# Whole-head probability-value products, PSUM tiles read when complete, and a new planned order in a two-layer attention and mLSTM trunk

## The chip, the cores and the metric

The kernel runs on one core of one Trainium2 chip. The metric is device time in microseconds (us), the median of three runs. The profile is of one execution; its span runs from the first to the last instruction on the core.

The engines are named as the profile names them: PE (TensorE, matmuls), PEld (its weight loads), DVE (VectorE), ACT (ScalarE), POOL (GpSimd) and SP (SyncE, which issues most of the transfers).

## What is computed

Two layers over 512 positions of width 1024. Each layer normalises its input, makes one combined projection and runs two branches from it; the output projection and the residual follow. Cut to what matters here:

```python
q = rope(rmsnorm(two_map_heads(aq), q_norm_g), cos, sin)      # 8 heads, two maps each, 64 wide
k = rope(rmsnorm(two_map_heads(ak), k_norm_g), cos, sin)
...
sc = jnp.einsum('bhqrd,bhkrd->bhrqk', qb, k) * scale           # per block of 128 queries
p = jax.nn.softmax(jnp.where(causal, sc, -jnp.inf), axis=-1)
a = p[:, :, 0] - lam * p[:, :, 1]
oa = jnp.einsum('bhqk,bhkd->bhqd', a, v)                       # v is 128 wide per head
oa = rmsnorm(oa, attn_norm_g) * (1.0 - lam_init) * jax.nn.silu(az)
ya = oa @ w_out_a
...                                                            # mLSTM branch: hb, yb
u = jax.nn.sigmoid(ga) * ya + jax.nn.sigmoid(gb) * yb
return x + u @ w_o
```

## The kernel before

**Number format.** A float32 operand is split into a high part and a remainder (ACT copies the high part, DVE subtracts it: `split`). A product of two such operands is three matmuls: high times high, high times remainder, remainder times high.

**Pieces and chains.** The weight products run as a list of pieces (`TUNE["order"]`): `qk` (queries and keys, four pairs of heads `c`), `av` (values), `az`, `ga`, `bo` and so on, mostly 512 columns wide. Around them stand chains of small steps: for each attention head `attn_head`, for each mLSTM head `ml_head`. Tiles of the profile carry these names: `qkt` are the transposed queries and keys of one pair and one block of 128 positions (four transposes into one PSUM tile, `qk_back`), `sc` the scores, `p` the probabilities, `ut` the transposed probabilities, `uh` and `ul` their high part and remainder, `msp` the sum of squares.

**A head's value products.** In the kernel before, `attn_head` makes them in two halves. `av(0)` covers query blocks 0 and 1 and `av(1)` blocks 2 and 3. Each product is 256 columns wide, and on the diagonal 128. The mLSTM products `num` are already made over the whole head, 512, 384, 256 and 128 columns wide for the four key blocks.

**Who sets the order.** The code does not issue its instructions in the order in which it is written. `Recorder.add` records each instruction with the earlier ones that it must follow. `Recorder.schedule` then plays a list scheduler over all engines, with a table of costs and a key for each instruction, and emits them in the planned order. Each engine runs its own instructions strictly in that order. The waits are then put in by the tile framework for the order that it was given. What the recorder does not know as a dependence, the scheduler may place in any order.

PSUM tiles come from small pools: one tile each for `tr` (all transposes, and the sums `msp`, `den`), `sc` (one of two banks) and `av`, four for the products of the pieces. A sum of squares or a denominator is added over the partitions with a matmul of ones: over two parts (high, remainder), or, for heads in `foldA`, `foldM` or `foldD`, over one part after the upper 64 partitions have been added onto the lower by DVE.

Of the kernel before, what the change touches and what calls it, by code (L numbers as in the profile page):

```python
# [18 lines left out]
P = 128  # L19
# [35 lines left out]
    "slack": 4130.0,
    "margin": 60.0,
    "pemargin": 48.4,
    "wait": 333.1,
    "swpen": 99746.2,
    "smargin": 0.2,  # L60
    "pwait": 2.0,
    "wdiff": 5762.0,
# [9 lines left out]
    "acl": 14,  # L72
    "gateA": 7,
    "gateM": 4,
    "actp": (0, 1, 2, 3),
    "m0": 217,
    "mp": 15,
    "m4": 17,
    "slots": 20,
    "bias": {'av': 11500.0, 'msp_a': -4400.0, 'wl': 2550.0, 'wo': -3700.0, 'mk': 6300.0, 'woh': -4650.0, 'wob': -850.0, 'bv': 2450.0, 'ht': 4400.0, 'woa': -1700.0, 'taz': -5550.0, 'sbo': -8700.0, 'wh': 7950.0, 'ga': -3100.0, 'ulZ': 7100.0, 'gt': -2650.0, 'qs': -5450.0, 'rq': -4050.0, 'p': -850.0, 'uz': -2750.0, 'x': -1750.0, 'ua': 5400.0, 'sdh': -3800.0, 'fo_b': -3100.0, 'lneps': 3350.0, 'wo1_P': 14300.0, 'qkt': -450.0, 'ml': 1700.0, 'den': -1900.0, 'sq': 3050.0, 'ulA': 10450.0, 'uhY': 1850.0, 'wo0_P': -850.0, 'cv': -2300.0, 'ulB': 8050.0, 'ob': 1850.0, 'gw': -150.0, 'out_0_dram': -3650.0, 'qss': 3500.0, 'gb': 100.0, 'xr': 1400.0, 'x1d': 5100.0, 'sinv': 5300.0, 'msl_a': 2200.0, 'p5_wo': -4150.0, 'saz': 3700.0, 's1_wo': 550.0, 'hh': -2400.0, 'mql': 1750.0, 'ulY': 9700.0, 'msp_b': 1200.0, 'em': -6750.0, 'sbz': -4900.0, 'wr': -2400.0, 'xn': 3500.0, 'posi': -500.0, 'ms': 12650.0, 'rot': 1400.0, 'sums': -1100.0, 'wt0_wo': 2350.0, 'mq': 650.0, 'uy': 100.0, 'qt': 5650.0, 'msh_d': 1700.0, 'gf': 1850.0, 'warm': -1450.0, 'ctab': 4550.0, 'gct': -4200.0, 'hl': 150.0, 'fo_a': 350.0, 'ones': 2100.0, 'fb_a': -700.0, 'ut': 450.0, 'ld': 5350.0, 'ang': -1900.0, 'mx': 5650.0, 'dq': 2300.0, 'uh': -500.0, 'gm': -550.0, 'fb_d': 1400.0, 'zeroc': 6400.0, 'gft': -100.0, 'bqk': 2050.0, 'gcol': -1000.0, 'oa': 500.0, 'sdl': 4250.0, 'uhB': 5750.0, 'tbz': 1150.0, 'cosv': 500.0, 'sc': 150.0, 'gi': 6100.0, 'msh_a': 400.0, 'uhA': 250.0, 'ss': 400.0, 'bo': 2500.0, 'posf': 2100.0, 'eps': -6650.0, 'fo_d': -2950.0, 'ws0_wo': -200.0, 'msh_b': -350.0, 'qk0_2x': 150.0, 'msl_d': -3500.0, 'junk': -900.0, 'epsc': 3000.0, 'fb_b': -100.0, 'kl': 1100.0, 'ks': -1450.0, 'msl_b': 200.0, 'ng': 550.0, 'rows': 150.0, 'gc': -150.0, 'qk1_0x': -500.0, 'qk1_2x': 100.0, 'stab': 650.0},  # L80
    "drain": 689.4,
    "risk": 335.5,
    "late": 278.0,
# [19 lines left out]
class Recorder:  # L103
# [61 lines left out]
    def add(self, eng, e, fn, a, k):  # L165
# [6 lines left out]
        for kind, aps in (("r", ins), ("w", outs)):  # L172
            for ap in aps:
                name, quad, mask = self.region(ap)
                ws, rs = self.acc.setdefault(name, ([], []))
                if kind == "r" and ap.space == PSUM:

                    for j, q, m in rs:
                        if self.ops[j]["eng"] != eng:
                            preds.setdefault(j, 0)  # L180
                if kind == "w":
                    for j, q, m in rs:
                        if q & quad and m & mask and j != i:
                            preds.setdefault(j, 0)
                    rs[:] = [x for x in rs if x[0] != i and (x[1] & ~quad or x[2] & ~mask)]
                for j, q, m in ws:
                    if q & quad and m & mask and j != i:
                        preds[j] = 1
                if kind == "w":
                    ws[:] = [x for x in ws if x[0] != i and (x[1] & ~quad or x[2] & ~mask)]  # L190
                    ws.append((i, quad, mask))
                else:
                    rs.append((i, quad, mask))
                t = self.tiles.get(name)
                if t is not None and (not t["ops"] or t["ops"][-1] != i):
                    t["ops"].append(i)
# [246 lines left out]
def kernel(ctx, tc, x, pos, wp, wg, cst, par, pb, ngb, out):  # L443
# [180 lines left out]
    def layer_events(l):  # L624
# [200 lines left out]
        def qk_done(c, tt, acc):  # L825
            if tt == 0:
                names = ("qs0", "qs1", "ks0", "ks1")
                if c % 2 == 0:
                    until(lambda: c == 0 or st.get(("A", 1), 0) > 6)
# [93 lines left out]
        def az_done(m, acc):  # L923
            if m > 1:
                until(lambda: st.get(("A", m - 2), 0) > 10)
            g = gp.tile([P, S], F32, tag="gate", name=f"saz{l}_{m}")
            silu2(g, acc, f"taz{l}_{m}")
            st[("az", m)] = g

        def bo_done(m, acc):  # L930
            until(lambda: st.get(("A", 6 + m), 0) > 10 if m < 2 else st.get(("M", m - 2), 0) > 5)
# [11 lines left out]
        def ga_done(m, acc):  # L943
            if "ua" not in st:
                until(lambda: st.get(("A", 5), 0) > 6)
                st["ua"] = big.tile([P, 8, S], F32, tag="big", name=f"ua{l}")
# [208 lines left out]

        def attn_head(h, t0):
# [33 lines left out]
            def tr(j):  # L1190
                pp, jj, n = j // 2, j % 2, P * (j + 1)
                if jj == 0:
                    loc["uh", pp] = t5([P, 4, 256], f"uh{l}_{h}_{pp}", F32R)
                    loc["ul", pp] = t5([P, 4, 256], f"ul{l}_{h}_{pp}", F32R)
# [3 lines left out]
                cs = slice(jj * P, (jj + 1) * P)  # L1198
                split(loc["uh", pp][:, : j + 1, cs], loc["ul", pp][:, : j + 1, cs], pst[:, : j + 1, :])

            def av(pp):
                if pp == 0:
                    loc["av"] = ps_av.tile([P, S], F32, tag="av", name=f"av{l}_{h}")
                o = loc["av"]
                uh, ul = loc["uh", pp], loc["ul", pp]
                kd = 2 * pp + 1
                c0 = 256 * pp

                def vv(k):
                    v = st[("av", g, k)]  # L1210
                    cs = slice((h % 4) * P, (h % 4) * P + P)
                    return v[:, 0, cs], v[:, 1, cs]

                full = list(range(kd))
                seq = []
                for k in full:
                    vh, vl = vv(k)
                    seq += [(vh, uh[:, k, :], 0), (vh, ul[:, k, :], 0), (vl, uh[:, k, :], 0)]
                vh, vl = vv(kd)
                dgn = [(vh, uh[:, kd, P:256], P), (vh, ul[:, kd, P:256], P), (vl, uh[:, kd, P:256], P)]  # L1220
                seq = seq[:1] + dgn + seq[1:]
                for i, (a, b, off) in enumerate(seq):
                    T.matmul(o[:, c0 + off : c0 + 256], a, b, start=i == 0, stop=i == len(seq) - 1, skip_group_check=True)
                if pp == 1 and h % 4 == 3:
# [12 lines left out]
            def msq():  # L1237
# [3 lines left out]
            fns = [lambda: qk(0), lambda: qk(1), lambda: tr(0), lambda: qk(2), lambda: tr(1), lambda: av(0), lambda: qk(3), lambda: tr(2),  # L1241
                   lambda: tr(3), lambda: (av(1), msq()), fin]

            def need(i):
                if i in (0, 1, 3, 6) and st.get(("qkn", c), 0) < (1, 2, 0, 3, 0, 0, 4)[i]:
                    return False
                if i == 5 and (("av", g, 3) not in st or st.get(("A", h - 1), 11) < 11):
                    return False
                return not (i == 10 and (("az", h) not in st or not room(1)))
# [47 lines left out]
        OFF = (0, 512, 1024, 896)  # L1297

        def ml_head(h, t0):
# [95 lines left out]
            def need(i):  # L1395
# [4 lines left out]
                if i == 4 and (("bv", grp, 3) not in st or st.get(("M", h - 1), 6) < 6 or st[("A", 7)] < 11):  # L1400
# [244 lines left out]
```

## Time and profile before

| | |
|---|---|
| median of 3 runs | 1344.62 us (1344.2 to 1345.06) |
| the profiled execution | 1344.67 us, of which the span is 1342.9 us |
| PE busy | 1331.3 us (99%), 6300 matmuls |
| DVE busy | 1012.6 us (75%) |
| ACT busy | 904.7 us (67%) |
| chain that ended last | PE 98%, ACT 1% |
| granted TensorE clock | 0.999 of full speed over the span |

A matmul's recorded duration overlaps with its neighbour's, so a product's cost is read from the distance between two starts. A row of the timeline gives the start, the duration, what ran, how many, and in brackets the idle time before it with what ended that.

### The profile page before, as it was taken

How to read it: one execution, taken by the hardware profiler on the slowest of the kernel's cores; microseconds unless marked ns; L12 is line 12 of the kernel's file. 1: busy time of each engine (PE TensorE's matmuls, PEld its weight loads, DVE VectorE, ACT ScalarE, POOL GpSimd, SP SyncE). 2: the span in 40 equal slices, each digit the busy share in tenths (PEclk: the TensorE clock that was granted, in tenths of full speed). 3: DMA queues.
4: the chain of work that ended last, by engine and by line, in shares of the span. 5: the costliest groups of instructions: out<-in, count | busy, mean ns of one | idle time of the engine just before them, and what ended most of it. 6: DMA issues, size and time to landing. Idle time of an engine off the chain costs nothing.

```text
span 1342.9 us, 17724 instructions
## 1 busy us (share of the span) xinstructions
PE 1331.3 (99%) x6300; PEld 1100.0 (82%) x6300; DVE 1012.6 (75%) x1806; ACT 904.7 (67%) x1828; POOL 36.9 (3%) x44
## 2 busy tenths in 40 slices
PE   8999999999999999999999999999999999999998
PEld 7787878888888888888888888788888888888887
DVE  7888988786549958755888888887754698587386
ACT  5787888885438858733668787888743488586243
POOL 1000000000000000000200000000000000000010
PEclk9999999999999999999999999999999999999999
DMA  5222222323244433455933122222322434434366
GB/s 186 87 79 64 79 78 64 94 77 101 91 119 112 132 108 114 137 136 146 265 104 97 53 95 63 79 63 94 99 82 91 120 107 135 128 109 140 121 190 172
DMA packets 51274, 148.17 MB, mean 110 GB/s; under 512 B 6096, under 2 KB 12880, under 8 KB 51184
## 3 DMA queue, kind: packets, MB, share of 16 engines
q1 hardware_dynamic: 48880, 138.63, 33.7%
q0 software_dynamic: 2304, 8.39, 3.5%
q8 instruction: 50, 0.82, 0.3%
q14 instruction: 40, 0.33, 0.1%
HBM read 142.74 MB, written 4.26 MB: 109 GB/s over the span
## 4 chain that ended last, share of the span: by engine, by line
PE 98%; ACT 1%; DMA 0%; DVE 0%; issue 0%; SPq 0%; DVEq 0%
PE qk L439 13%; PE av L439 9%; PE az L439 7%; PE ga L439 7%; PE bv L439 7%; PE bo L439 7%; PE bz L439 7%; PE woa L439 7%; PE gb L439 7%; PE bqk L439 7%; PE wob L439 6%; PE wo_P L439 6%; PE sc L439 3%; PE num L439 2%; PE ms L439 1%; PE ut L439 1%
## 5 line engine op out<-in xcount | busy, mean ns | idle before, releaser
L439 ACT CAST wh<-wr 128x1024 fp32r<-128x1024 f32 (+1 forms) x206 | 214.9, 1045 | 195.8 <-PE woa L439 37.7
L439 DVE TENSOR_TENSOR wl<-wr,wh 128x1024 fp32r<-128x1024 f32 x204 | 249.0, 1221 | 108.5 <-ACT wh L439 105.7
L439 PE MATMUL qk<-wl,hh 128*128 128x512 f32 x256 | 94.1, 398 | 0.7 <-DVE wl L439 0.7
L439 PE MATMUL qk<-wh,hl 128*128 128x512 f32 x256 | 93.8, 400 | 0.1
L439 PE MATMUL qk<-wh,hh 128*128 128x512 f32 x256 | 93.3, 399 | 0.6 <-ACT hh L439 0.6
L439 PE MATMUL woa<-oa,wh 128*128 128x512 f32 x256 | 88.5, 391 | 0.0
L439 PE MATMUL wob<-ob,wh 128*128 128x512 f32 x256 | 83.4, 389 | 0.0
L439 ACT ACTIVATE p<-sc,mx,rq 128x128 f32<-128x128 f32 (+3 forms) x128 | 78.9, 618 | 6.5 <-DVE mx L439 6.0
L438 ACT ACT_TABLE_LOAD x61 | 78.3, 1283 | 1.1
L439 PEld LDWEIGHTS qk<-wl,hh 128*128 128x128 f32 x256 | 47.9, 188 | 10.6 <-DVE wl L439 1.2
L439 PEld LDWEIGHTS wob<-ob,wh 128*128 128x128 f32 x256 | 48.1, 188 | 10.0
L439 PEld LDWEIGHTS qk<-wh,hl 128*128 128x128 f32 x256 | 48.0, 188 | 9.7 <-DVE hl L439 0.4
L439 PEld LDWEIGHTS woa<-oa,wh 128*128 128x128 f32 x256 | 47.8, 188 | 9.7
L439 PEld LDWEIGHTS qk<-wh,hh 128*128 128x128 f32 x256 | 47.7, 188 | 9.5 <-ACT hh L439 0.9
L439 DVE TENSOR_REDUCE mx<-sc 128x2 f32<-128x256 f32 (+1 forms) x64 | 52.5, 821 | 0.9
L439 PE MATMUL az<-hh,wl 128*128 128x512 f32 x128 | 51.3, 401 | 0.0
L439 PE MATMUL az<-hl,wh 128*128 128x512 f32 x128 | 50.9, 398 | 0.0
L439 PE MATMUL ga<-hh,wl 128*128 128x512 f32 x128 | 50.6, 398 | 0.0
L439 PE MATMUL ga<-hh,wh 128*128 128x512 f32 x128 | 50.5, 395 | 0.0
L439 PE MATMUL az<-hh,wh 128*128 128x512 f32 x128 | 50.5, 397 | 0.0
L439 PE MATMUL ga<-hl,wh 128*128 128x512 f32 x128 | 50.4, 394 | 0.0
L439 PE MATMUL woa<-oa,wl 128*128 128x512 f32 x128 | 50.0, 391 | 0.0
(314 smaller groups left out, 3737.7 us busy)
## 6 DMA issues: line engine op xcount, KB each, us to landing
wr<-in_wp_dram SPq DMA_DIRECT2D x204, 512.0 KB, 3.6
ws_wo<-in_wp_dram POOLq DMA_DIRECT2D x12, 512.0 KB, 6.6
dd<-rows SPq DMA_DIRECT2D x16, 256.0 KB, 4.9
em<-rows SPq DMA_DIRECT2D x16, 256.0 KB, 3.9
dd<-rows SPq DMA_DIRECT2D x16, 192.0 KB, 5.4
x<-in_x_dram SPq DMA_DIRECT2D x4, 512.0 KB, 8.5
dd<-rows SPq DMA_DIRECT2D x16, 128.0 KB, 6.2
ws_wo<-in_wp_dram SPq DMA_DIRECT2D x4, 512.0 KB
```

Source lines behind the costliest of these rows:

```text
L438: self.tc.keep_in_program_order(self.nc.scalar.preload_act_table_set(self.SET_NAME[o["load"]]))
L439: self.tc.keep_in_program_order(getattr(o["e"], o["fn"])(*o["a"], **o["k"]))
```

## The change

Four things change.

1. In `Recorder.add`, an instruction that reads a PSUM tile now follows every product or transpose recorded so far for that bank of the tile, whatever part of it is read.
2. `attn_head` makes a head's value products once for the whole head, as `num` does: four key blocks of 512, 384, 256 and 128 columns, three matmuls each. `uh` and `ul` are one tile per head. The last block's transposes are copied out in two pieces.
3. Sets in `TUNE`: head 6 leaves `foldA`, all heads are in `foldD`, the scaling of `p` for query block 1 moves from ACT to DVE (`actp`), and the first four pieces split their remainder in two halves (`wsp`).
4. Nearly every number of `TUNE` that feeds the scheduler changes, among them the list of pieces, and so does the order on all engines.

```diff
-    "attn": (1, 5, 5, 8, 9, 10, 12, 16, 16, 19, 24),
+    "attn": (1, 5, 5, 8, 9, 13, 15, 16, 19, 24),
...
-    "pemargin": 48.4,
+    "pemargin": 171.8,
...
-    "wsp": 0,
+    "wsp": 4,
...
-    "foldA": (2, 3, 5, 6),
+    "foldA": (2, 3, 5),
     "foldM": (0, 1, 2, 3, 4, 7),
-    "foldD": (0, 1, 3, 5, 6),
+    "foldD": (0, 1, 2, 3, 4, 5, 6, 7),
...
-    "actp": (0, 1, 2, 3),
+    "actp": (0, 2, 3),
...
                 for j, q, m in ws:
-                    if q & quad and m & mask and j != i:
+
+                    whole = kind == "r" and ap.space == PSUM and any((m >> b) & 0xFFFF and (mask >> b) & 0xFFFF for b in (0, 16))
+                    if (whole or q & quad and m & mask) and j != i:
                         preds[j] = 1
...
             def tr(j):
...
+                uh, ul = (loc[n].rearrange("p (b c) -> p b c", c=P) for n in ("uh", "ul"))
+                bs = slice(j, j + 3 * min(j, 2) + 1, 3)
+                split(uh[:, bs, :], ul[:, bs, :], pst[:, : min(j, 2) + 1, :])
+                if j == 3:
+                    split(uh[:, 7, :], ul[:, 7, :], pst[:, 3, :])
+
+            def av():
+                loc["av"] = o = ps_av.tile([P, S], F32, tag="av", name=f"av{l}_{h}")
+                seq = []
+                for k in range(NT):
                     v = st[("av", g, k)]
                     cs = slice((h % 4) * P, (h % 4) * P + P)
+                    us = slice(OFF[k], OFF[k] + S - P * k)
+                    vh, vl, uh, ul = v[:, 0, cs], v[:, 1, cs], loc["uh"][:, us], loc["ul"][:, us]
+                    seq += [(k, vh, uh), (k, vh, ul), (k, vl, uh)]
+                seq = seq[:1] + seq[2:] + seq[1:2]
+                for q, (k, a, b) in enumerate(seq):
+                    T.matmul(o[:, P * k :], a, b, start=q == 0, stop=q == len(seq) - 1, skip_group_check=True)
+                if h % 4 == 3:
                     give(4)
```

The first place is on PE in layer 0: the four transposes of `qkt0_1_1` (layer 0, pair 1, block 1). Before:

```order
L439 MATMUL av0_1_272<-ul0_1_1_308,av0_0_3_209 128x128
L439 MATMUL av0_1_272<-uh0_1_1_307,av0_0_3_209 128x128
L439 MATMUL qkt0_1_1_312<-ct_94,rot0_1_1_287 128x128 [waits DVE_49,PE_49]
L439 MATMUL qkt0_1_1_312<-ct_94,rot0_1_1_287 128x128 x2
L439 MATMUL qkt0_1_1_312<-ct_94,rot0_1_1_287 128x128 [waits Activation_49]
L439 MATMUL sc0_2_0_322<-kl10_1_281,qs10_1_277 128x128 [waits Pool_49]
```

And now:

```order
L441 MATMUL av0_1_314<-uh0_1_257,av0_0_2_208 128x256
L441 MATMUL av0_1_314<-ul0_1_258,av0_0_2_208 128x256
L441 MATMUL qkt0_1_1_307<-ct_94,rot0_1_1_286 128x128 [waits DVE_49,PE_49]
L441 MATMUL qkt0_1_1_307<-ct_94,rot0_1_1_286 128x128 x3
L441 MATMUL sc0_2_0_318<-kl10_1_280,qs10_1_276 128x128 [waits Pool_49]
```

The fourth transpose no longer waits for ACT: all four stand together behind one wait.

The second place is on PE in layer 0, the value products of head 5 (`av0_5`; behind the arrow stand the probabilities and the values of one key block). Before, the second half of the head:

```order
L439 MATMUL av0_5_551<-uh0_5_1_577,av0_1_0_371 128x256 [waits Activation_49]
L439 MATMUL av0_5_551<-uh0_5_1_577,av0_1_3_381 128x128
L439 MATMUL ga0_4_595<-hl0_115,wh36_574 128x512
L439 MATMUL ga0_4_595<-hh0_114,wl36_575 128x512
L439 MATMUL av0_5_551<-ul0_5_1_578,av0_1_3_381 128x128 [waits DVE_49]
L439 MATMUL av0_5_551<-uh0_5_1_577,av0_1_3_381 128x128
L439 MATMUL av0_5_551<-ul0_5_1_578,av0_1_0_371 128x256
L439 MATMUL av0_5_551<-uh0_5_1_577,av0_1_0_371 128x256
L439 MATMUL av0_5_551<-uh0_5_1_577,av0_1_1_372 128x256
L439 MATMUL av0_5_551<-ul0_5_1_578,av0_1_1_372 128x256
L439 MATMUL av0_5_551<-uh0_5_1_577,av0_1_1_372 128x256
L439 MATMUL av0_5_551<-uh0_5_1_577,av0_1_2_373 128x256
```

And now, the whole head but its first product:

```order
L441 MATMUL av0_5_568<-uh0_5_531,av0_1_0_364 128x512
L441 MATMUL av0_5_568<-uh0_5_531,av0_1_1_365 128x384
L441 MATMUL az0_7_590<-hl0_115,wh36_564 128x512
L441 MATMUL av0_5_568<-ul0_5_532,av0_1_1_365 128x384 [waits DVE_49]
L441 MATMUL av0_5_568<-uh0_5_531,av0_1_1_365 128x384
L441 MATMUL av0_5_568<-uh0_5_531,av0_1_2_366 128x256
L441 MATMUL av0_5_568<-ul0_5_532,av0_1_2_366 128x256
L441 MATMUL av0_5_568<-uh0_5_531,av0_1_2_366 128x256
L441 MATMUL av0_5_568<-uh0_5_531,av0_1_3_375 128x128 [waits Activation_49]
L441 MATMUL av0_5_568<-ul0_5_532,av0_1_3_375 128x128 [waits DVE_49]
L441 MATMUL av0_5_568<-uh0_5_531,av0_1_3_375 128x128
L441 MATMUL av0_5_568<-ul0_5_532,av0_1_0_364 128x512
```

Eighteen products in two groups have become twelve in one, with waits for ACT and DVE at the start of the group and again at its last key block.

## Rows read from the trace of the kernel before

**Rows 1.** The page: the span, the busy time of three engines (share, instructions) and the chain that ended last, by engine.

```profile
span 1342.9 us, 17724 instructions
...
PE 1331.3 (99%) x6300; PEld 1100.0 (82%) x6300; DVE 1012.6 (75%) x1806; ACT 904.7 (67%) x1828; POOL 36.9 (3%) x44
...
PE 98%; ACT 1%; DMA 0%; DVE 0%; issue 0%; SPq 0%; DVEq 0%
```

**Rows 2.** The waits of PE: for whom, us in total, times, the longest.

```profile
PE qkt L439 <- ACT qk_2x L439: 1.8, 4, 0.5
PE qkt L439 <- ACT qs L439: 1.8, 4, 0.5
...
PE qkt L439 <- ACT qk_0x L439: 0.5, 1, 0.5
```

**Rows 3.** The timeline of PE and ACT around one such wait (`qkt` of layer 0, pair 2, block 1).

```profile
181.00 0.49 PE L439 MATMUL qkt<-ct,rot 128*128 128x128 f32 x3
181.53 0.36 ACT L439 CAST qk_2x<-qkt 64x256 fp32r<-64x256 f32 x1 [0.93 <-PE qkt L439]
...
181.94 0.33 PE L439 MATMUL qkt<-ct,rot 128*128 128x128 f32 x1 [0.45 <-ACT qk_2x L439]
```

**Rows 4.** The timeline of PE at two groups of `qkt` with other products between their transposes (pair 1, block 0; pair 3, block 0): the third and the fourth transpose of each. Two 512-column products stand between the two rows of either pair.

```profile
107.81 0.27 PE L439 MATMUL qkt<-ct,rot 128*128 128x128 f32 x1
...
108.68 0.30 PE L439 MATMUL qkt<-ct,rot 128*128 128x128 f32 x1
...
220.33 0.27 PE L439 MATMUL qkt<-ct,rot 128*128 128x128 f32 x1
...
221.06 0.33 PE L439 MATMUL qkt<-ct,rot 128*128 128x128 f32 x1
```

**Rows 5.** The timeline of PE at value products of head 7, layer 0, in two stretches with nothing else between them: six products (three of 256 columns, three of 128), then ten (two of 128 columns, eight of 256). Shown are the first and the last row of each and what follows.

```profile
296.93 0.34 PE L439 MATMUL av<-uh,av 128*128 128x256 f32 x2
...
297.50 0.28 PE L439 MATMUL av<-uh,av 128*128 128x256 f32 x1
297.62 0.39 PE L439 MATMUL bv<-wl,hh 128*128 128x512 f32 x1
...
307.58 0.22 PE L439 MATMUL av<-ul,av 128*128 128x128 f32 x1
...
308.63 0.28 PE L439 MATMUL av<-uh,av 128*128 128x256 f32 x1
308.75 0.40 PE L439 MATMUL woa<-oa,wh 128*128 128x512 f32 x1
```

**Rows 6.** The same view of the mLSTM products `num` of head 7, layer 0: twelve in one stretch, three each of 512, 384, 256 and 128 columns. The first and the last row, and what follows.

```profile
560.16 0.80 PE L439 MATMUL num<-sdh,bv 128*128 128x512 f32 x3
...
561.78 0.45 PE L439 MATMUL num<-sdl,bv 128*128 128x512 f32 x1
562.07 0.62 PE L439 MATMUL wob<-ob,wh 128*128 128x512 f32 x2
```

**Rows 7.** The chain that ended last, in order of time: an undisturbed stretch of 512-column products (start, us, what).

```profile
998.17 8.61 PE bqk L439 x38
```

**Rows 8.** Timeline of PE, ACT and DVE: the shortest reuse of the PSUM tile `tr`, from a transpose through its two copies to the next transpose.

```profile
727.45 0.30 PE L439 MATMUL ut<-ct,p 128*128 128x128 f32 x1
...
727.78 0.27 ACT L439 CAST uh<-ut 128x128 fp32r<-128x128 f32 x1 [1.06 <-PE ut L439]
...
728.13 0.28 DVE L439 TENSOR_TENSOR ul<-ut,uh 128x128 fp32r<-128x128 f32 x1
...
728.61 0.38 PE L439 MATMUL ut<-ct,p 128*128 128x128 f32 x2
```

**Rows 9.** Groups of instructions by line, engine and operation: count, busy us and mean ns, then the idle time before them.

```profile
L439 ACT CAST wh<-wr 128x1024 fp32r<-128x1024 f32 (+1 forms) x206 | 214.9, 1045 | 195.8 <-PE woa L439 37.7
L439 DVE TENSOR_TENSOR wl<-wr,wh 128x1024 fp32r<-128x1024 f32 x204 | 249.0, 1221 | 108.5 <-ACT wh L439 105.7
...
L438 ACT ACT_TABLE_LOAD x61 | 78.3, 1283 | 1.1
...
L439 ACT ACTIVATE p<-p,sums 128x256 f32<-128x256 f32 x16 | 8.2, 512 | 2.3 <-DVE sums L439 2.3
...
L439 ACT CAST uh<-ut 128x384 fp32r<-128x384 f32 x16 | 7.6, 475 | 2.0 <-PE ut L439 2.0
...
L439 ACT COPY fb_d<-dd 64x512 f32<-64x512 f32 x10 | 6.2, 620 | 6.1 <-DVE dd L439 5.9
...
L439 DVE TENSOR_TENSOR dd<-dd,fb_d 64x512 f32<-64x512 f32 x10 | 6.8, 681 | 0.0
...
L439 DVE TENSOR_TENSOR rot<-rot,rq 128x256 f32<-128x256 f32 x16 | 6.7, 420 | 0.3
...
L439 DVE TENSOR_TENSOR ul<-ut,uh 128x128 fp32r<-128x128 f32 x16 | 4.6, 287 | 2.5 <-ACT uh L439 2.5
```

**Rows 10.** Busy time of each engine in the attention stretch of layer 0 (from and to in us, its length, then PE, PEld, DVE, ACT, POOL, the granted clock, the DMA share and GB/s).

```profile
45.00:180.00 135.00, 133.95 (x675) 110.00 (x674) 118.86 (x265) 108.11 (x291) 2.85 (x3) 1.00 0.23 72
```

**Rows 11.** The timeline of PE at the start of the program: the first products that wait for a remainder, and a transpose that waits for the normalised input.

```profile
10.67 0.50 PE L439 MATMUL qk<-wl,hh 128*128 128x512 f32 x1 [0.27 <-DVE wl L439]
...
12.87 0.63 PE L439 MATMUL ht<-ct,junk 128*128 128x128 f32 x4 [0.40 <-DVE junk L439]
...
14.58 0.50 PE L439 MATMUL qk<-wl,hh 128*128 128x512 f32 x1 [0.41 <-DVE wl L439]
```

More of the change, by code (lines that the diff above doesn't have):

```diff
@@ L71 @@
     "prods": 'P1 P5 P3 P6 P2 P7 P4',
[L72 to L76 removed]
+    "acl": 12,
+    "gateA": 9,
+    "gateM": 0,
+    "actp": (0, 2, 3),
+    "m0": 218,
     "mp": 15,
[L78 removed]
+    "m4": 11,
     "slots": 20,
[L80 removed]
@@ L81 @@
-    "drain": 689.4,
-    "risk": 335.5,
-    "late": 278.0,
+    "bias": {'av': 27450.0, 'msp_a': -4350.0, 'wl': 2400.0, 'wo': -3700.0, 'woh': -4650.0, 'ht': 29150.0, 'taz': -4050.0, 'ga': 16050.0, 'gt': -8800.0, 'p': -300.0, 'wo1_P': 23900.0, 'out_0_dram': -5900.0, 'p5_wo': -4950.0, 'rot': 12650.0, 'dq': -4400.0, 'oa': 450.0, 'dd': 30900.0, 'num': 20100.0, 'ld': -4700.0, 'ws1_wo': -1200.0, 'gw': -1100.0, 'hl': -350.0, 'sc': -1400.0, 'uz': -3750.0, 'mk': 7250.0, 'sbz': 550.0, 'az': 10300.0, 'posi': -650.0, 'msl_d': 1650.0, 's1_wo': 1700.0, 'wob': 50.0, 'msh_d': 6450.0, 'sq': -1600.0, 'warm': 3150.0, 'bo': -400.0, 'sdl': 200.0, 'ml': 15800.0, 'fo_b': 11200.0, 'ws0_wo': -900.0, 'wt1_wo': 1300.0, 'pb': 2000.0, 'sbo': 5350.0, 'qkt': 2000.0, 'junk': 6150.0, 'ulZ': 7650.0, 'bv': 650.0, 'bqk': -1750.0, 'uh': -3950.0, 'ms_b': -1550.0, 'gi': 1000.0, 'ob': 250.0, 'uy': 1750.0, 'gcol': -750.0, 'ms': 11250.0, 'cosv': -4100.0, 'ms_a': 1450.0, 'ones': 2450.0, 'msh_b': 6650.0, 'x1d': -1650.0, 'qt': 1100.0, 'qk0_2x': -6300.0, 'fb_a': 4650.0, 'saz': 900.0, 'xr': -2300.0, 'fb_b': 900.0, 'wo0_P': 450.0, 'qk1_0x': 1950.0, 'fb_d': -5800.0, 'msh_a': 2700.0, 'ulA': -150.0, 'ang': 150.0, 'rnh': 1400.0, 'gft': 6600.0, 'gct': 200.0, 'gc': -300.0, 'mql': -1200.0, 'rows': 150.0, 'kl': -700.0, 'posf': -150.0, 'zw': 2400.0, 'qk1_2x': -3000.0, 'gf': 450.0, 'qk0_0x': -50.0, 'uhY': 7150.0, 'qs': 3050.0, 'qy': 250.0, 'ul': -500.0, 'msl_a': 2800.0, 'uhZ': 7800.0, 'lneps': -950.0, 'gm': -4350.0, 'lq': 450.0, 'x': -3700.0, 'eps': -700.0, 'sgb': 150.0, 'wr': -400.0, 'wt0_wo': -300.0, 'stab': 8000.0, 'xn': 1200.0, 'qss': 150.0, 'den': 2000.0, 'msl_b': 950.0, 'rn': -150.0, 'glf': 900.0, 'ss': 4250.0, 'bz': -100.0, 'sdh': -200.0, 'em': -250.0, 'uhB': 850.0, 'rq': 250.0, 'sinv': -1650.0},
@@ L84 @@
+    "drain": 251.9,
+    "risk": 295.5,
+    "late": 912.7,
 }
@@ L828, in qk_done @@
                 if c % 2 == 0:
-                    until(lambda: c == 0 or st.get(("A", 1), 0) > 6)
+                    until(lambda: c == 0 or st.get(("A", 1), 0) > 5)
                     xt = big.tile([P, 8, S], F32R, tag="big", name=f"qk{l}_{c}x")
@@ L924, in az_done @@
             if m > 1:
-                until(lambda: st.get(("A", m - 2), 0) > 10)
+                until(lambda: st.get(("A", m - 2), 0) > 9)
             g = gp.tile([P, S], F32, tag="gate", name=f"saz{l}_{m}")
@@ L944, in ga_done @@
             if "ua" not in st:
-                until(lambda: st.get(("A", 5), 0) > 6)
+                until(lambda: st.get(("A", 5), 0) > 5)
                 st["ua"] = big.tile([P, 8, S], F32, tag="big", name=f"ua{l}")
@@ L1153, in chain @@
                 at(t0 + dt, step(i))
+        OFF = (0, 512, 1024, 896)
         def attn_head(h, t0):
@@ L1399, in need @@
                     return False
-                if i == 4 and (("bv", grp, 3) not in st or st.get(("M", h - 1), 6) < 6 or st[("A", 7)] < 11):
+                if i == 4 and (("bv", grp, 3) not in st or st.get(("M", h - 1), 6) < 6 or st[("A", 7)] < 10):
                     return False
```

62 lines of the change are left out of this document (19 added, 43 removed), and 8 rows, old and new, of the table TUNE.

## The prediction

> **What bounds the kernel now.** I read the page first. PE is busy 1331.3 of 1342.9 us, and the chain that ended last is 98% PE [rows 1]. A busy PE may still be a waiting one, so the view of PE's waits comes next. It lists nine waits of PE before a `qkt` transpose for an ACT copy out of a `qkt` tile, 4.1 us in all [rows 2]. That is no wait for data, since a transpose reads `rot` and not `qkt`. The timeline shows what it is. Three transposes start at 181.00, 181.11 and 181.22 us (three of them span 0.49, a single one 0.27), ACT begins to copy the same tile at 181.53, and the fourth transpose starts at 181.94 only when that copy is done [rows 3]. The recorder lets a copy that reads columns 0 to 255 stand before the last transpose, which writes other columns, and in the built order that transpose waits for the copy. So the time is PE's work, plus a few stops that the order itself makes. The change touches both.
>
> **The value products.** The widths add up to 3840 columns per head before and after; only the number of products falls, from 18 (12 of 256 columns, 6 of 128) to 12 (three each of 512, 384, 256 and 128). Two undisturbed stretches give the price before. Three products of 256 and three of 128 take 297.62 - 296.93 = 0.69 us; eight of 256 and two of 128 take 308.75 - 307.58 = 1.17 us [rows 5]. Solved for the two, a 256 costs 0.118 us and a 128 costs 0.112 us: half the columns save next to nothing. A head costs 12 x 0.118 + 6 x 0.112 = 2.09 us. The new form is that of `num`, whose twelve products took 562.07 - 560.16 = 1.91 us [rows 6]. The difference is 0.18 us a head, for 16 heads **2.9 us less**.
>
> The Trainium skill (TensorE: Matmul & The Clock Gate, Back-to-back issue gap) gives an isolated gap of N/2.4 + 2.5 ns for N columns. By it a 128 would cost 56 ns where the row shows 112, and six products fewer at equal columns would save 15 ns a head, 0.24 us in all; the sum below would lose 2.7 us of its gain. The rows disagree with it at this width, and they decide.
>
> **The folded sums.** A folded sum is one product of ones where the other is two. Three more heads fold `den` and one fewer folds `msp_a`, in both layers: (3 - 1) x 2 = 4 products of 512 columns fewer. 38 such products took 8.61 us, 0.227 each [rows 7]: **0.9 us less**.
>
> **The transposes that waited for a reader.** In the new order none of the copies out of a `qkt` tile stands between its transposes. The fourth transpose at 181.94 started 0.72 us after the third where 0.11 is normal: 0.61 lost, nine times [rows 2, 3], **5.5 us**. Four more groups have other products between their transposes and wait less. From 107.81 to 108.68 there are 0.87 us for one transpose and two products, 0.11 + 2 x 0.227 = 0.56, so 0.31 is lost; from 220.33 to 221.06 there are 0.73, so 0.17 is lost [rows 4]. Each has its like in layer 1: 2 x 0.31 + 2 x 0.17 = **1.0 us**. The price is that a copy may start a transpose or two (0.11 us each) later. ACT and DVE are off the path there, and what follows the copies is the scores, several products later. Some transposes still wait for ACT, those of blocks 0 and 2, whose keys ACT scales; those waits were there before, at the same places, and cost nothing that the waits view shows.
>
> **What it adds.** All of this is beside PE. DVE gets six additions for the folds (0.681 each), 16 scalings of `p` (no row shows that form; at most a two-input operation of the size, 0.420) and 16 small remainders (0.287): 4.1 + 6.7 + 4.6 = 15 us at most. ACT loses 8.2 us of scalings and gets six copies of 0.620, four table loads of 1.283 and the 16 small copies, for which I take DVE's 0.287: 3.7 + 5.1 + 4.6 - 8.2 = 5 us [rows 9]. DVE is busy 118.86 of 135 us in the attention stretch of layer 0, ACT 108.11 [rows 10]; some 11 of DVE's 15 us fall in the two attention stretches, on well over 400 us, and lift it from 88 to about 91%. I cost this at nothing. The cover is PE's own queue; where DVE reaches the length of PE's work, each us comes through.
>
> **New short distances.** Reusing the tile `tr` after one transpose took 728.61 - 727.45 = 1.16 us, and that is the nearest row for any quick turn of PE, ACT, DVE, PE [rows 8]. In the new order the sum `msp_a` of heads 1 and 4 in each layer follows four products behind the one transpose of a `ut` tile, 0.11 + 4 x 0.227 = 1.02 us: 0.14 lost, four times, **0.5 us more**. The lower bound for all other new waits is zero, since the planner was given a larger distance for PE (`pemargin`); the upper one is in the second rival.
>
> **The start.** The first products wait for a remainder (0.27 and 0.41 us), and halves of it come earlier. But between them a transpose waits for the input's norm (0.40), which the halves don't move [rows 11]. Bounds: nothing to 0.7 us less. I take nothing, because that transpose is the last to come.
>
> **The sum.** 2.9 + 0.9 + 5.5 + 1.0 - 0.5 = 9.8 us less. The profiled execution took 1344.67 us (span 1342.9 and 1.8 around it), 0.05 above the median. So 1344.67 - 9.8 = **1334.9 us**.
>
> **Rivals.** *The stops move.* PE no longer stops at `qkt`, but runs into ACT or DVE a little later, since both are near their fill. For it: DVE's 88%. Against it: in that stretch PE waits 1.05 us of 135 [rows 10], so the queues kept up. It leaves the smaller work alone: 1344.67 - 2.9 - 0.9 = 1340.9 us.
>
> *The head's end becomes the stop (slower).* A whole head's products must wait for the last block's probabilities, where half of them used to go ahead. By the new order 12 of the 16 heads have only five to eight products between the last transpose and the first value product, 0.11 + 5 x 0.227 = 1.25 us or more. The chain under it is 0.33 until ACT starts, 0.475 for the copy and 0.20 back to PE [rows 8, 9], 1.0 us. If ACT has a weight copy of 1.045 us ahead of it, PE stops for some 0.6 us (0.8 at five products, 0.4 at seven). If DVE has a weight remainder of 1.221 ahead of `ul` too, the first three products (0.63) don't hide it: 0.6 more. Twelve heads at 1.2 us are 14 us: 1334.9 + 14 = 1349 us. It decides from 9.8 / 12 = 0.8 us a head. Against it: before, the same copies stood as close, and no wait of PE for `uh` or `ul` is among its waits of 0.3 us or more.
>
> *The reading rule does nothing.* The waits come from the framework and not from the recorder, so other transposes could wait instead; with small losses elsewhere the time stays within 0.2% (2.7 us, about what a measurement of this kernel can tell from no change): 1344 us. Against it: the rows of the new order show one wait where there were two.
>
> *Columns alone count.* If narrow products cost by their columns, the first term falls to 0.2: 1334.9 + 2.7 = 1337.6 us, the result that the section named above would give. Against it: [rows 5].
>
> **Chances.** The forecast 66%, between 1332 (the start and some small older waits also gone) and 1337; columns alone 3%; the stops move 14%; the head's end 9%; nothing nets 8%. Faster by over 0.2%: 0.66 + 0.03 + 0.14 = 0.83; within: 0.08; slower: 0.09. The range runs from 1331 to 1342: it takes in the moved stops and leaves out the last two cases, 17%.
>
> **What would show it.** Right: no `qkt` among PE's waits; four `qkt` transposes 0.11 us apart; twelve value products in about 1.9 us where they stand together; 6200 matmuls; a PE chain of 98% or more. Wrong: waits of PE for `uh`, `ul`, `wh` or `wl` in the attention stretches, above all before the first or the fourth value product of a head, or DVE at 95% there.

## The result, and the profile of the changed kernel

The changed kernel takes **1334.61 us** (median of 4 runs, 1334.22 to 1334.73); the kernel before took 1344.57 us beside it (4 runs, 1344.2 to 1345.06). The ratio is 0.9925, with a 95% interval of 0.9908 to 0.9942. The forecast was 1334.9 us. The profiled execution took 1334.56 us, its span is 1332.5. One of the four executions of the reading rule alone, further down, took 1893.5 us at a granted clock of 0.65; the numbers given there are of the other three.

From the page of the changed kernel: its span and instructions, the busy time of each engine with its share and instructions, and the shares of the chain that ended last (they answer to [rows 1]).

```profile
span 1332.5 us, 17532 instructions
...
PE 1325.0 (99%) x6200; PEld 1095.0 (82%) x6200; DVE 1018.0 (76%) x1846; ACT 907.8 (68%) x1836; POOL 36.9 (3%) x44
...
PE 98%; ACT 1%; DMA 0%; SPq 0%; DVE 0%; issue 0%; DVEq 0%
```

PE has 100 products fewer and is still the chain. All of PE's waits that the view of [rows 2] lists (what PE waited for: us in total, times, the longest):

```profile
PE warm L441 <- DVE ml L441: 1.6, 1, 1.6
PE qk L441 <- ACT hh L441: 0.5, 1, 0.5
PE ht L441 <- DVE junk L441: 0.5, 2, 0.3
PE qk L441 <- DVE wl L441: 0.5, 1, 0.5
PE wo_P L441 <- ACT p_wo L441: 0.3, 1, 0.3
PE wo_P L441 <- ACT wh L441: 0.3, 1, 0.3
```

The nine waits of `qkt` are gone. No wait names `uh` or `ul`. One is new: `wo_P` for `p_wo`. The timeline shows the group of pair 2, block 1 in layer 0, which was [rows 3] before. All four transposes stand in one row, 0.60 us for the four, and ACT's copy of the tile starts behind them:

```profile
176.21 0.60 PE L441 MATMUL qkt<-ct,rot 128*128 128x128 f32 x4
...
176.84 0.36 ACT L441 CAST qk_2x<-qkt 64x256 fp32r<-64x256 f32 x1 [0.52 <-PE qkt L441]
```

The value products of head 2, where one of the three 512-column products stands ahead and eleven products together (start, us, the product, how many; a row that merges several shows the shape of its first):

```profile
146.12 0.40 PE L441 MATMUL av<-uh,av 128*128 128x512 f32 x1
146.36 0.39 PE L441 MATMUL sc<-ks,qs 128*128 128x256 f32 x2
...
146.82 0.58 PE L441 MATMUL av<-uh,av 128*128 128x512 f32 x2
147.24 0.34 PE L441 MATMUL av<-ul,av 128*128 128x384 f32 x1
147.41 0.47 PE L441 MATMUL av<-uh,av 128*128 128x384 f32 x2
147.72 0.28 PE L441 MATMUL av<-ul,av 128*128 128x256 f32 x1
...
148.24 0.44 PE L441 MATMUL av<-ul,av 128*128 128x512 f32 x1
148.52 0.62 PE L441 MATMUL qk<-wh,hh 128*128 128x512 f32 x2
```

The first took 146.36 - 146.12 = 0.24, the eleven 148.52 - 146.82 = 1.70: 1.94 us for the head, where `num` took 1.91 [rows 6]. The windows of two stretches follow (us, then busy time and instructions of PE, PEld, DVE, ACT and POOL, granted clock, DMA share, GB/s); the first is that of [rows 10].

```profile
45.00:180.00 135.00, 135.00 (x669) 111.62 (x669) 121.85 (x284) 110.05 (x303) 2.84 (x3) 1.00 0.23 75
...
635.00:690.00 55.00, 54.66 (x255) 44.19 (x254) 44.74 (x69) 32.44 (x59) 8.20 (x9) 1.00 0.65 190
```

In the first stretch PE waited 1.05 us before and does not wait now; DVE went from 118.86 to 121.85 of 135 us, ACT from 108.11 to 110.05. The second stretch holds the new wait.

**Where the time went.** I add up both traces product by product: the distance from one start on PE to the next, less a price for the product's width (0.227 us for 512 columns, 0.173 for 384, 0.120 for 256, 0.1075 for 128). What is over is lost time. The stretches have the same bounds in both traces, though the changed kernel comes to be up to 10 us further along in its work.

| lost on PE, us | before | changed | difference |
|---|---|---|---|
| price of the products | 1311.2 | 1307.1 | -4.1 |
| start, 0 to 50 us | 6.2 | 5.2 | -1.1 |
| attention, 50 to 250 and 700 to 900 us | 13.8 | 6.6 | -7.2 |
| last heads, 250 to 300 and 900 to 950 us | 1.4 | 2.2 | +0.8 |
| output products, 600 to 700 us and from 1300 us | 1.3 | 2.4 | +1.1 |
| the rest | 3.4 | 3.5 | +0.1 |

The sum is 10.4 us, the difference of the spans. The measured times differ by 10.0.

The 0.8 us of the last heads lie mostly at two places in each layer, the sums `msp_a` of heads 5 and 6. In layer 0 the first starts at 262.21, 0.37 us behind the product ahead of it instead of 0.227, and the product behind it 0.31 later; at head 6 it is 0.30 and 0.30 (288.15, 288.45, 288.75). That is 0.38 us more than the price in each layer.

### The profile page after: what moved, and what is told of

Read it like the earlier page. It is cut to its first block, busy times and chain, and to the rows that moved or that the text cites. A ratio compares the mean times of both kernels' runs of the same rounds, so it can differ in the third digit from the quotient of the medians.

```text
span 1332.5 us, 17532 instructions
## 1 busy us (share of the span) xinstructions
PE 1325.0 (99%) x6200; PEld 1095.0 (82%) x6200; DVE 1018.0 (76%) x1846; ACT 907.8 (68%) x1836; POOL 36.9 (3%) x44
## 4 chain that ended last, share of the span: by engine, by line
PE 98%; ACT 1%; DMA 0%; SPq 0%; DVE 0%; issue 0%; DVEq 0%
PE qk L441 13%; PE av L441 9%; PE az L441 7%; PE bv L441 7%; PE bqk L441 7%; PE bz L441 7%; PE bo L441 7%; PE gb L441 7%; PE ga L441 7%; PE woa L441 7%; PE wob L441 7%; PE wo_P L441 6%; PE sc L441 3%; PE num L441 2%; PE ms L441 1%; PE ut L441 1%
## 5 line engine op out<-in xcount | busy, mean ns | idle before, releaser
L441 DVE TENSOR_TENSOR wl<-wr,wh 128x1024 fp32r<-128x1024 f32 (+1 forms) x208 | 248.9, 1200 | 99.7 <-ACT wh L441 98.9
L441 PE MATMUL qk<-wh,hh 128*128 128x512 f32 x256 | 96.1, 401 | 0.5 <-ACT hh L441 0.5
L441 PE MATMUL bqk<-hh,wl 128*128 128x512 f32 x128 | 50.3, 393 | 0.0
L441 PE MATMUL bo<-hh,wl 128*128 128x512 f32 x128 | 50.2, 392 | 0.0
L441 PE MATMUL bo<-hl,wh 128*128 128x512 f32 x128 | 50.1, 391 | 0.0
L441 PE MATMUL bo<-hh,wh 128*128 128x512 f32 x128 | 50.0, 391 | 0.0
L441 PE MATMUL bqk<-hl,wh 128*128 128x512 f32 x128 | 50.0, 393 | 0.0
L441 PE MATMUL gb<-hl,wh 128*128 128x512 f32 x128 | 49.8, 392 | 0.0
```

The source lines that it names most:

```text
L441: self.tc.keep_in_program_order(getattr(o["e"], o["fn"])(*o["a"], **o["k"]))
```

## The experiments

Times are medians; the kernel before ran between them and took 1344.4 to 1344.9. **One part at a time** comes first, then the order as a whole, then how close the new order stands to its next stops.

The *reading rule* is the first of the four changes. *Order numbers* are the fourth, the numbers of `TUNE` that feed the scheduler. *Whole heads* are the second, *halves* the value products as they were. *Planned anew* means that the scheduler made a new order for the edited code; *in its own order* means that the order was kept.

**The stops alone.** In the kernel before, each transpose into a `qkt` tile is issued ahead of the copies that read the tile. On PE four of them move by one or two places; the order on the other engines stays as it was:

```
         for i in order:
...
+            for j in sorted(self.ops[i]["ahead"]):
+                if j not in done and all(k in done for k in self.ops[j]["pre"]):
+                    done.add(j)
+                    seq.append(j)
...
+            seq.append(i)
```

`ahead` lists the writers of a `qkt` tile that were recorded before a copy that reads the tile.

> The kernel before, its planned order untouched on ACT, DVE, SP and POOL. On PE only four qkt transposes move, one or two places forward; elsewhere the transposes are merely emitted ahead of the copy that reads their tile, so that they no longer wait for it. My theory (the stops are reads between transposes, and PE's time comes back one for one): 6.5 us less than before, 1338.1 us (1337.3 to 1339), no qkt among PE's waits. The rival (the stops move to ACT or DVE, which are near full): 1343 to 1344.6 us, with new waits of PE in the attention stretches. A second rival (the gain of the change is the new planned order alone): 1344.6 us.

Measured: 1340.28 us (1339.88 to 1340.43, ratio 0.9966, 0.9953 to 0.9978). No `qkt` is left among PE's waits. Product by product against the kernel before, each of the nine stops gives back 0.61 to 0.69 us, and the four groups with other products between their transposes 0.33 and 0.21, 1.1 together. The mechanism and both prices hold. But some 2.5 us come back as small delays, mostly six to eight us behind a removed stop: 0.20 near 122.4, 0.24 near 194.5, 0.38 near 232.5 of the trace before, 0.14 and 0.16 ahead of two other groups of transposes (114.6 and 225.9), and their likes in layer 1. One of them, on PE and ACT of this kernel:

```profile
229.24 0.39 PE L452 MATMUL az<-hl,wh 128*128 128x512 f32 x1
229.47 0.39 PE L452 MATMUL az<-hh,wl 128*128 128x512 f32 x1
229.97 0.50 PE L452 MATMUL sc<-qk_2x 128*128 128x256 f32 x2
```

```profile
229.37 0.46 ACT L452 ACTIVATE p<-sc,mx,rq 128x128 f32<-128x128 f32 x1
229.73 0.19 ACT L452 ACTIVATION_READ_ACCUMULATOR p<-sc,mx,rq 128x1 f32 x1
```

`az` starts at 229.47, the scores 0.50 behind it where 0.23 is normal. They start 0.05 us after ACT has finished with `p` (229.73 + 0.19 = 229.92), which reads the scores made ahead of them. 0.27 is lost there, and 0.25 at the like of it near 891 us; the other delays were not traced to what they wait for. The attention stretches lose 9.1 us in this kernel, 13.8 before and 6.6 in the changed one: a part of the rival "the stops move" is true when only the stops are taken out.

**The width of the products.** The changed kernel in its own order; each product of 512 and 384 columns is issued as two:

```
+            if n in (512, 384):
...
+                cut = n - 256
+                first = dict(o["k"], stop=False)
+                self.tc.keep_in_program_order(o["e"].matmul(d[:, :cut], w, m[:, :cut], **first))
+                self.tc.keep_in_program_order(o["e"].matmul(d[:, cut:], w, m[:, cut:], **dict(o["k"], start=False)))
```

> The changed kernel in its own order, but each 512- and 384-column value product of a head is emitted as two (256 and 256, 128 and 256 columns): the widths of before, 96 products more, the same columns. My theory (a product of 128 costs nearly what one of 256 does): 2.9 us more than the changed kernel, 1337.5 us (1337 to 1338). The rival (columns alone count): 1334.8 us.

Measured: 1338.23 us (1337.77 to 1339.73), 3.6 more than the changed kernel and 0.2 above the range of the theory, with no new wait over 0.2 us. That is 0.038 us for each of the 96 added products at equal columns. By the isolated gap of the Trainium skill (TensorE: Matmul & The Clock Gate, Back-to-back issue gap), which the same section says under-counts narrow products in a stream with weight loads, they would have cost an estimated 0.24 us together; the measurement is fifteen times that.

**The halves under the new order numbers.** The value products in halves as before, with the reading rule and the new numbers and sets, planned anew. A head then has one more step, so the list of its steps gets one more place. Part of the edit, against the changed kernel:

```
-    "attn": (1, 5, 5, 8, 9, 13, 15, 16, 19, 24),
+    "attn": (1, 5, 5, 8, 9, 10, 13, 15, 16, 19, 24),
...
-                    loc["uh"] = t5([P, 1280], f"uh{l}_{h}", F32R)
...
+                    loc["uh", pp] = t5([P, 4, 256], f"uh{l}_{h}_{pp}", F32R)
```

> The new order numbers and the reading rule, but the probabilities times values in two halves per head as before (18 products of 256 and 128 columns instead of 12 of 512 to 128; one more step in the list of a head's steps, and the order planned anew for it). Theory (the price of the products is the width's, a 128 as dear as a 256): 16 heads x 0.18 = 2.9 us more than the changed kernel, 1337.5 us (1336.5 to 1339), no new wait of PE for qkt. Rival (columns alone count; the halves cost nothing): 1334.6 to 1335. Rival (whole heads cost a stop at the head's end that the halves avoid): below 1334.6. Over 1340: the new order numbers fit the whole heads only, and the planned order is then what differs.

Measured: 1341.53 us (1340.41 to 1342.77), 6.9 more than the changed kernel and past the 1340 from which the expectation puts the difference down to the order. The trace's own sum: 3.2 for the products, nearly as expected (2.9), and 3.2 of lost time beside them. One of its waits is new (0.9 us of `msp_a` for `msh_a`), the rest is small. The order that the planner makes for one more step costs as much as the products.

**The reading rule alone**, in the kernel before with its old numbers:

```
-                    if q & quad and m & mask and j != i:
+
+                    whole = kind == "r" and ap.space == PSUM and any((m >> b) & 0xFFFF and (mask >> b) & 0xFFFF for b in (0, 16))
+                    if (whole or q & quad and m & mask) and j != i:
```

> The kernel before with the reading rule alone, planned anew with the old numbers. If the rule alone brings what the qkt stops cost: 1338.1 us. But the plan changes with it, and in the built order head 5 of each layer has its first value product right behind the transposes that it reads, and two transposes of ut close behind a copy. Priced by the copies (0.4 to 0.7 and the way back), some 2.5 us for each layer: 1343 us (1341 to 1345). That the planned order decides as much as the rule is the theory of the second; the first says 1338.

Measured: 1356.55 us (1354.97 to 1356.59, ratio 1.0083), **11.7 slower** than before. It removes the `qkt` stops of [rows 2], though a new one for `kl` comes in each layer (1.4 us), and the attention stretches lose less, 11.0 instead of 13.8. But the planner answers to the rule with another order, and near the end of each layer's attention PE stops twice. The main waits of PE, and PE at the place in layer 0:

```profile
PE ut L441 <- DVE ul L441: 3.5, 2, 1.7
PE qkt L441 <- DVE kl L441: 2.8, 2, 1.4
PE av L441 <- DVE ms_a L441: 2.2, 2, 1.1
```

```profile
252.09 0.42 PE L441 MATMUL av<-uh,av 128*128 128x256 f32 x2 [1.10 <-DVE ms_a L441]
...
255.46 1.11 PE L441 MATMUL ut<-ct,p 128*128 128x128 f32 x4 [1.73 <-DVE ul L441]
...
256.80 0.63 PE L441 MATMUL ga<-hl,wh 128*128 128x512 f32 x1
257.23 0.63 PE L441 MATMUL ga<-hh,wl 128*128 128x512 f32 x1
```

```profile
250.00:256.00 6.00, 3.14 (x21) 2.37 (x20) 5.36 (x12) 5.95 (x12) 0.00 (x0) 0.89 0.04 13
256.00:262.00 6.00, 6.00 (x18) 4.75 (x17) 3.33 (x9) 4.10 (x10) 0.00 (x0) 0.54 0.28 87
```

The last block has the windows around it (columns as in [rows 10]). The stops are not all of the price. From 256 to 262 us PE is full, but the granted clock is 0.54 of full speed, about the lower of the two levels (1.2 of 2.4 GHz): the products of 512 columns start 0.43 us apart instead of 0.23. The last-heads stretches lose 14.2 us, 1.4 before.

**The changed kernel without the rule**, planned anew:

```
-                    if (whole or q & quad and m & mask) and j != i:
+                    if q & quad and m & mask and j != i:
```

> The changed kernel without the reading rule, planned anew with the same numbers. In the built order eight qkt and nine ut transposes then stand behind a copy that reads their tile, and some six more one product away. My theory: 8 x 0.61, 9 x 0.7 and 6 x 0.4 us, 14 us more than the changed kernel, 1348 us (1345 to 1350), slower than before. The rival (such stops are absorbed elsewhere): 1335 to 1338 us.

Measured: 1365.71 us (1364.83 to 1366.75, ratio 1.0155), 31 us more than with it. Among PE's waits:

```profile
PE ut L439 <- ACT uh L439: 5.6, 11, 0.6
PE az L439 <- DVE wl L439: 5.2, 2, 2.7
PE qkt L439 <- ACT qk_2x L439: 2.3, 6, 0.5
```

The `ut` tiles are now hit as the `qkt` tiles were (eleven waits of 0.5 us), and DVE is late with weight remainders, 5.2 us in two waits; that DVE was pushed back by the other stops is likely and not shown. The whole is more than the price of the stops, and more than either theory gave.

**The new code with the old order numbers**, planned anew. The sets of the third change stay the new ones. Part of the edit:

```
-        "qk0 av0 gate az0 qk1 az1 az2 av1 qk2 az3 az4 qk3 az6 ga3 az5 ga5 ga4 ga2 az7 bqk7 bv0 bqk4 bqk1 "
...
+        "qk0 av0 gate az0 qk1 az1 az2 av1 qk2 az3 az4 qk3 ga0 az6 ga7 az5 ga3 ga2 ga4 az7 bv0 woa3 woa4 "
...
-    "margin": 72.0,
-    "pemargin": 171.8,
+    "margin": 60.0,
+    "pemargin": 48.4,
```

> The changed kernel's code (whole heads, reading rule, its folds and steps) with the order numbers of before: order of the groups, biases, margins and places of steps. Theory (rule and whole heads give their 2.9 + 0.9 us, but the order numbers are what keeps the stops away; without new ones PE stops anew): 1340 to 1356 us, with waits of PE for copies (ut, av, qkt, ul) in the list of its waits that the changed kernel does not have. Rival (the order numbers are worth nothing by themselves; whole heads and rule do it all): 1334 to 1336.

Measured: 1356.57 us (1356.1 to 1356.93, ratio 1.0089), 22 more than the changed kernel. The largest of the new waits:

```profile
PE ut L441 <- DVE ul L441: 6.3, 4, 1.8
```

So the parts don't add up one by one. In the first two kernels the sets of the third change (`foldA`, `foldD`, `actp`, `wsp`) are the old ones, in the other four the new:

| order numbers | rule | products | us |
|---|---|---|---|
| old | no | halves (the kernel before) | 1344.6 |
| old | yes | halves | 1356.6 |
| old | yes | whole heads | 1356.6 |
| new | no | whole heads | 1365.7 |
| new | yes | halves | 1341.5 |
| new | yes | whole heads (the changed kernel) | 1334.6 |

With the rule, the new numbers are worth 22 us to the whole heads, and together with the new sets 15 us to the halves. The whole heads are worth 6.9 us under the new numbers; under the old they gain nothing even with the new sets beside them, though their products are cheaper there too. Of the sets only `wsp` was run by itself, next.

**The start.** The first weights' remainders in one piece, as before, planned anew:

```
-    "wsp": 4,
+    "wsp": 0,
```

> The changed kernel with the first weights' remainders made in one piece as before instead of in halves (one number; apart from that some products of the first 30 us swap places). Theory (the first products wait for these remainders, and the halves are what the start gained): 0.5 to 1.0 us more, 1335.1 to 1335.6. Rival (the start's gain came from the order of the transfers or differs from run to run): 1334.4 to 1334.8.

Measured: 1340.12 us (1338.45 to 1340.42), 5.5 more. The start took 0.8 us longer than in the changed kernel's trace (lost time 6.0 against 5.2). The rest came from a place 120 us later, where the planner, led to another order by this number, let PE wait 2.4 us for `mx`; here too the clock fell behind it:

```profile
PE ut L441 <- DVE mx L441: 2.4, 1, 2.4
```

```profile
146.00:149.00 3.00, 1.68 (x9) 1.35 (x10) 2.94 (x8) 2.92 (x9) 0.00 (x0) 0.99 0.00 0
149.00:152.00 3.00, 3.00 (x11) 2.71 (x10) 2.59 (x8) 1.21 (x2) 0.00 (x0) 0.50 0.00 0
```

For the start this settles little. The last transposes of the start (`ht`) begin at 22.03 us in the kernel before and 21.35 in the changed one, but kernels with the changed one's very order of the start had them later: at 21.75 to 22.10 in the three kernels below, and with the narrow products at 22.70. After the changed kernel's row comes that of the narrow products:

```profile
21.35 0.60 PE L441 MATMUL ht<-ct,junk 128*128 128x128 f32 x4
```

```profile
22.70 0.60 PE L450 MATMUL ht<-ct,junk 128*128 128x128 f32 x4
```

In the execution with the narrow products the granted clock was 0.51 from 12 to 15 us; in the changed kernel's and the other three it was 1.00 there, and these still differ by up to 0.75 us. So between profiled executions of one order the start moves by 0.75 us at full clock and by 1.35 in all, as much as the 1.1 us of the table.

**Late copies.** How much cover there is at a head's end: in the changed kernel's own order ACT copies the last block's `uh` three times. Part of the edit:

```
+            again = 2 if o["kind"] == "uh" and o["eng"] == "ACT" and len(o["a"][1].shape) == 3 and o["a"][1].shape[1] == 3 and id(o) in self.last else 0
+            for _ in range(again):
+                self.tc.keep_in_program_order(getattr(o["e"], o["fn"])(*o["a"], **o["k"]))
```

> The changed kernel in its own order, with one edit: ACT copies the last block's transposed probabilities (uh, 0.475 us) three times instead of once in each of the 16 heads, so they are ready 0.95 us later and ACT has 15.2 us more work. Theory (the cover at a head's end is only five to eight products, 1.25 to 1.9 us, for a chain of 1.0 us): about 12 heads stop for 0.5 to 0.6 us each, 6 to 7 us, 1341 us (1338 to 1344), and PE's waits name uh in front of the first or fourth value product. Rival (the products recorded there give more cover than that, and what I called the head's end is far from deciding): below 1336. Rival (ACT was near its fill and the 15.2 us come through in full): 1348 to 1350, with stops at other places than the heads' ends.

Measured: 1347.67 us (1347.4 to 1348.91), 13.1 more. Product by product against the changed kernel, **twelve** heads stop in front of value products, by 0.25 to 0.98 us and 8.4 us together; that is the expected place, count and nearly the size. Six groups of `qkt` transposes behind that copy stop too, for 0.7 to 0.9 us each, 4.7 us together, which I had not counted. Head 5 of layer 0, ACT, then PE:

```profile
258.51 0.98 ACT L444 CAST uh<-ut 128x384 fp32r<-128x384 f32 x2
...
259.31 0.40 PE L445 MATMUL ga<-hl,wh 128*128 128x512 f32 x1
...
259.53 0.48 ACT L445 CAST uh<-ut 128x384 fp32r<-128x384 f32 x1
...
260.06 0.92 PE L445 MATMUL av<-uh,av 128*128 128x512 f32 x3 [0.36 <-ACT uh L445]
```

The time lies nearest to the rival "fill", though the places are the theory's. The next run was made to tell these two apart.

**Early copies.** About the same amount of ACT work (16.8 us; the late copies added 15.2), on the first block's copy. Part of the edit, against the changed kernel:

```
+            again = 4 if o["kind"] == "uh" and o["eng"] == "ACT" and id(o) in self.last else 0
...
+                if j == 0:
+                    rec.last.update(id(x) for x in rec.ops[-2:])
```

> The counterpart of the late copies: the changed kernel in its own order, but it is the first block's copy (uh of 128 columns, 0.263 us) that ACT makes five times instead of once in each of the 16 heads, some 1 us per head and 16.8 us of ACT work in all, a little more than the late copies added. Between that copy and the last block's ACT is idle, by the changed kernel's trace, 1.4, 5.0, 0.9, 4.2, 1.5, 0.1, 1.7 and 3.6 us in heads 0 to 7 of layer 0, and as much in layer 1. Theory (place: only what pushes the last block's copy back costs PE): heads 2 and 5 of each layer are pushed by 0.1 and 0.9 us, the rest not, so 2 us in all, and a little at other places: 1335 to 1338. Rival (fill: ACT has no room, so its added time comes through wherever it stands): 1346 to 1350, as with the late copies.

Measured: 1351.51 us (1351.06 to 1351.96), 16.9 more. My theory missed by 14 us; the rival "fill" is nearer, 1.5 us above its range. But ACT is not full: in the stretch of [rows 10] it is busy 110.95 of 135 us in this kernel. Each of the 16 heads stops 0.7 to 1.3 us, within some microseconds of that copy, and PE is then as late as ACT, so no head's end stops. The largest of the new waits, then PE, ACT and DVE at one of them, and then the same place in the changed kernel:

```profile
PE msp_a L445 <- DVE ul L445: 8.3, 8, 1.2
PE sc L445 <- ACT p L445: 2.6, 5, 0.8
```

```profile
133.73 0.27 PE L445 MATMUL ut<-ct,p 128*128 128x128 f32 x1
...
134.04 1.16 ACT L444 CAST uh<-ut 128x128 fp32r<-128x128 f32 x4 [0.78 <-PE ut L445]
...
135.53 0.29 DVE L445 TENSOR_TENSOR ul<-ut,uh 128x128 fp32r<-128x128 f32 x1 [1.36 <-ACT uh L445]
...
135.87 0.50 PE L445 MATMUL msp_a<-msh_a,ones 128*128 128x512 f32 x1 [0.94 <-DVE ul L445]
```

```profile
131.17 0.27 PE L441 MATMUL ut<-ct,p 128*128 128x128 f32 x1
...
131.48 0.27 ACT L441 CAST uh<-ut 128x128 fp32r<-128x128 f32 x1 [0.78 <-PE ut L441]
...
131.78 0.29 DVE L441 TENSOR_TENSOR ul<-ut,uh 128x128 fp32r<-128x128 f32 x1 [0.16 <-ACT uh L441]
...
132.21 0.41 PE L441 MATMUL msp_a<-msh_a,ones 128*128 128x512 f32 x1
```

`msp_a` takes the tile that the `ut` transpose filled, so it needs the remainder `ul` to have read it. In the changed kernel this turn takes 132.21 - 131.17 = 1.04 us and ends just when PE arrives. With the copies 1.16 us later, PE stops for 1.1. Before the copies ACT stood idle for 0.78 us, waiting for PE's transpose: no backlog of ACT made this stop. It is the short turn of PE, ACT, DVE and PE that I had put down at four places [rows 8]. The eight waits of `msp_a` for `ul` are this turn; at the other heads PE stops mostly for the probabilities `p`, a fold or the next transpose. ACT was idle ahead of the copy at six heads (0.65 to 1.74 us); at the other ten it came straight from other work, and what held PE there was not taken apart further. Since every head stops for 0.7 us or more of the 1.16 added, this place has less than half a microsecond to spare at all of them.

**The new wait, taken away.** In the changed kernel's own order, on ACT one weight copy `wh` goes behind the two copies `p_wo` in layer 0. Part of the edit:

```
+        order.insert(b + 1, w)
+        del order[a]
```

> The changed kernel in its own order with one instruction moved on ACT: in the wo stage of layer 0 the copy of one weight tile (wh, 1.06 us, at 639.84) goes behind the two copies p_wo, so that these are made when their products are done. Theory (the new wait of PE for p_wo at 641.9 us is that order's, 0.6 us): 0.6 us less, 1334.0, and p_wo gone from PE's waits. Rival (the weight copy is then late and PE waits for it instead): 1334.6 or more, with a wait for wh or wl near 645 us.

Measured: 1334.92 us (1334.57 to 1335.28), 0.3 more, which is no clear difference. The stop at 641.9 us is gone (some 0.6 us regained), but the weight remainder is late 3 to 5 us further on and costs 1.0, of which 0.4 come back by 658 us. Nothing is gained, as the rival said; the wait of the changed kernel can't be had back by this move.

```profile
646.94 0.50 PE L448 MATMUL wo_P<-wl,uhZ 128*128 128x512 f32 x1 [0.29 <-DVE wl L448]
```

## Why the prediction was right, and where it was not

**The bound** held: PE's chain is 98% before and after.

**The value products and the folded sums**: forecast 2.9 + 0.9 = 3.8, found 4.1 by the trace; the narrow products confirm the price of a product in the chip's time (3.6 for 96 of them; 2.9 was expected). The rival "columns alone count" is out.

**The transposes that waited**: forecast 5.5 + 1.0. The stops alone gave 0.61 to 0.69 for each of the nine, and the four split groups 1.1, so both terms were sized right. What the terms left out is that the other engines then have less time, and some 2.5 us came back when nothing else changed; at the one place that was traced, PE came before ACT was done with `p`. In the new order they do not come back: the attention stretches improve by 7.2, 0.7 more than the terms' 6.5. That better order I did not foresee.

**The additions beside PE**: forecast nothing, and PE does not wait in the stretch of [rows 10]. DVE is busy 90% there (forecast 91). Over the whole kernel DVE's busy time grew by 1018.0 - 1012.6 = 5.4 us (forecast 15 at most) and ACT's by 3.1 (forecast 5): what the folds and the new copies take away on these engines was left out of the forecast.

**The short distances**: forecast 0.5 lost for four turns at 0.14 each; found 0.04 each. The turn takes 1.04 us there, not the 1.16 of [rows 8]. But the sum `msp_a` loses 0.38 us in each layer at heads 5 and 6, which I had not put down; that loss is counted below.

**The start**: taken as nothing, and 1.1 us earlier in the one profiled execution; the same start moved by 0.75 us between profiled executions at full clock and by 1.35 with one that lost it, so I can't say how much of it is the halves.

**All other new waits**: I took the lower bound, zero. The output products and the last heads lost 1.9 us more: the wait for `p_wo`, the sums of heads 5 and 6, and smaller ones. This is the step that failed. By luck the start (1.1) and the attention stretches (7.2, where 6.5 - 0.5 was forecast) outweighed it, and neither gain was foreseen, so the sum is nearer than its parts: -3.8, -6.5, +0.5, 0 and 0 were forecast, -4.1, -7.2 (the short distances within it), -1.1, +1.9 and +0.1 found.

**The rival of the head's end** did not come about, but the price that I worked out for it was real. Twelve heads have the cover that I read from the order, and the copies 0.95 us later cost 8.4 us there. The changed kernel is spared because its order brings ACT to that copy in time, even at head 4, where two weight copies stand directly ahead of it: I had taken such a copy for a stop of 0.6 us.

**The reading rule**: my text said what the rule does to the order that was built, and that was right. Any reading of it as a part with its own price is wrong: by itself, with the old numbers, it costs 11.7 us.

## What to carry to other kernels

Where a planner sets the order, cost the built order, not the edits. The reading rule cost 12 us with the old numbers and saved 31 with the new ones, and the whole heads saved 7 or nothing, while the places in the finished order could be read to some tenths of a microsecond. When a stop is taken out, look at what the other engines did during it: that work can be late next, as `p` was. And to learn how close a full engine's order is to stopping, make one copy on a helper engine longer at one place and see where the wait appears; here a microsecond of it came through nearly whole at two places, though the changed kernel shows no wait at either.

## What the runs showed of the hardware

A stop of PE can cost more than its length. After PE had been busy 3.14 of 6 us (the rule alone) and 1.68 of 3 us (the start's remainders in one piece), the granted clock in the windows that followed was 0.54 and 0.50 with PE full, and a 512-column product took 0.43 us instead of 0.23. In the first case that added some 3 us to two stops of 3.2 together in each layer. The nine stops of 0.61 us before, and the sixteen of about 1 us with the early copies, did not bring it down: the mean granted clock of those two executions is 0.999 and 1.000.
